# A gated feed-forward's up-projection, with eight block products per unit or seven

## The chip, the cores and the metric

The kernel runs on one core of a Trainium2 chip. The metric is the time of one execution on the device, in microseconds (us). The core has five instruction streams that run side by side and meet at semaphores: TensorE (PE in the profile, its weight loads PEld), VectorE (DVE), ScalarE (ACT), GpSimd (POOL) and SyncE (SP), which issues the DMAs.

## The reference

One layer of a hybrid encoder on 1024 prompt rows and 8 × 16 sample rows, 1152 rows in all, of width 1024. Attention, a pooling branch and gates come first and are not touched. The change is in the feed-forward part:

```python
h2 = rmsnorm(x, norm_ffn)
up = h2 @ w_up                                   # (1152, 1024) @ (1024, 5632)
c, conv_new = causal_dwconv(up, conv_left, conv_w, conv_b)   # width 3 along the rows
gate, val = jnp.split(c, [D_FF], axis=-1)        # D_FF = 2816
x = x + (jax.nn.gelu(gate) * val) @ w_down       # (2816, 1024)
```

All data is float32. The kernel holds each matmul operand as two parts of type fp32r, `hi` (a rounded copy) and `lo` (the rest), and adds three matmuls: hi·hi, hi·lo and lo·hi (`mm3`, lines 120 to 123).

## The kernel before

The stages follow one another: input norm and pooling branch, projections and attention, the sample rows' attention, gates and output projection (to 893 us), up-projection (893 to 1446 us), down-projection (to the end).

The normalised input of the feed-forward lies transposed in SBUF: `mh0`/`ml0` hold rows 0 to 383, `mh12`/`ml12` rows 384 to 1151, each as 8 k-blocks of 128 channels. The up-projection (`up_unit`, lines 1303 to 1333) goes over 22 units m. A unit makes 128 gate columns (u = m) and 128 value columns (u = 22 + m). For each, `load_col` fetches the 1024 × 128 weight block, ACT makes its hi part and POOL its lo part (line 98); TensorE then makes three chunks of 384 rows, in the order 1, 2, 0, each 8 k-blocks × 3 matmuls into a PSUM bank. ACT copies each chunk to E (line 1320) and, scaled, to C (line 1321); DVE adds the two other convolution taps (lines 1324 and 1325, 128 sample and 1024 prompt columns); then GELU on ACT, the product with the value half on DVE (line 1332), and a store to DRAM (`sp_g`). Weight blocks have three buffers.

The down-projection runs over 18 units, one for each half of the 22 g blocks and each tile of 128 rows. Two units share each pass over the weight blocks where blocks are still arriving (units 0 and 1, 7 and 8, 9 and 10); the others run alone. `wd_load` fetches a block of w_down and splits it, `g_load` a tile of g. PSUM there has the tags `tp` and `pj`, two banks each, one tag for each half of the output columns; line 1396 adds a finished half to the residual.

The Tile framework orders the instructions of each engine before the program runs, by its own reckoning and by program order, and places the semaphores. Inside `manual_schedule` the order is the written one; the down-projection has that for TensorE alone, the up-projection not.

Of the kernel before, what the change touches and what calls it, by code (L numbers as in the profile page):

```python
# [25 lines left out]
NU = DFF // P  # L26
# [13 lines left out]
def trunk_kernel(  # L40
# [15 lines left out]
    def f32(ap):  # L56
        return ap.bitcast(F32)

    def mk_pool(name, side=None, space=None, stack=ctx):
        kw = dict(name=name, bufs=1)  # L60
        if space is not None:
            kw["space"] = space
        if side is not None:
            kw["side"] = side
        if space != DRAM:
            kw["reuse_waits"] = "tile"
        return stack.enter_context(tc.tile_pool(**kw))
# [120 lines left out]
        for _, fn in fill[i:]:  # L188
            fn()

    psp = mk_pool("ps", space=PSUM)
    ZT = ("z", 3)
    TT = ("tp", 2)

# [1044 lines left out]
    convp = fcp.tile([P, 4, 2 * NU + 4], F32, name="convp")  # L1239
    convs = fcp.tile([P, 2 * NU, 16], F32, name="convs")  # L1240
    convq = fcp.tile([P, 64, 2], F32, name="convq")[:, :2 * NU, :]


    s5 = ExitStack()
# [57 lines left out]
    EA = -(-EL // HD) * HD  # L1302
    def up_unit(m):
        cc = []
        for s_ in range(2):
            u = s_ * NU + m
            wt = load_col(w_up3, u * P, f"wup{u}")
            E = p6.tile([P, EA], F32, tag="E", bufs=3, name=f"E{u}")
            C = p6.tile([P, T], F32, tag="C", bufs=3, name=f"C{u}")
            pool.memset(E[:, EZ:EP], 0.0)  # L1310
            pool.tensor_copy(E[:, 0:16], sconvT[:, u, :])
            for c in CORD:
                cs = slice(c * CH, (c + 1) * CH)
                ps = psp.tile([P, CH], F32, tag="z", bufs=3, name=f"up{u}_{c}")
# [7 lines left out]
            for tap, sh in ((1, 1), (0, 2)):  # L1322
                wv = convp[:, tap, u:u + 1]
                dve.scalar_tensor_tensor(C[:, 0:P], E[:, 16 - 8 * sh:EZ - 8 * sh], wv, C[:, 0:P], ALU.mult, ALU.add)  # L1324
                dve.scalar_tensor_tensor(C[:, P:T], E[:, EP - sh:EL - sh], wv, C[:, P:T], ALU.mult, ALU.add)  # L1325
            pool.tensor_copy(convs[:, u, :].rearrange("p (b j) -> p j b", j=2),
                             E[:, P:EZ].rearrange("p (j b) -> p j b", b=NB))
            pool.tensor_copy(convq[:, u, :], E[:, EL - 2:EL])
            cc.append(C)
        act.activation(cc[0], cc[0], AF.Gelu_apprx_tanh)  # L1330
        g = p6.tile([P, T], F32, tag="g", bufs=2, name=f"g{m}")
        dve.tensor_tensor(g, cc[0], cc[1], ALU.mult)
        sync.dma_start(sp_g[:, m, :], g)

    def conv_out(rows, n, stores, nm):
        ps = psp.tile([P, P], F32, tag="av", bufs=1, name=f"tr_{nm}")
        tc.keep_in_program_order(pe.transpose(ps[:n, :], rows, ident))
        st = pa.tile([P, P], F32, tag="cst", bufs=2, name=nm)
# [22 lines left out]

    def wd_load(m):
        i = m % NH
        alt = (wp, "hi", "lo", 3) if i < 3 else (pa, "dh", "dl", PA) if i < 3 + PA else \
            (pb, "dh", "dl", NH - 3 - PA)
        src = w_down[0, m * P:(m + 1) * P, :]
        wds[m] = load_w(lambda r: [(r, src)], [D], f"wd{m}", "ad" if i % 2 else "ap", alt)

    def g_load(u, parts=1):
        h, t = UNITS[u]  # L1370
        gq = pa if u % 4 < 2 else pb
        gh, gl = [gq.tile([P, NH, P], F32R, tag=f"gg{i}", bufs=2, name=f"g{u}_{i}") for i in range(2)]
        raw = pa.tile([P, NH, P], F32, tag="graw", bufs=2, name=f"g{u}_r")
# [26 lines left out]
    def final_half(t, hf):  # L1400
        hs = slice(hf * 512, (hf + 1) * 512)
        if hf == 0:
            fin[t] = [p8.tile([P, D], F32, tag=tg, bufs=2, name=f"{tg}{t}") for tg in ("yo", "xg")]
# [16 lines left out]
    for m in range(NU):  # L1420
        up_unit(m)
        if m in (8, 16):
            conv_rows(0, m - 8)
            conv_rows(1, m - 8)
        if m == 17:
            for q in range(3, 3 + PA):
                wd_load(q)
            g_load(0)
            g_load(1)
    s_m.close()  # L1430
    pb = mk_pool("pb", "right")
    for q in (0, 1, 2, *range(3 + PA, NH)):
        wd_load(q)
    s6.close()
    p8 = mk_pool("p8", "left")
    gfin = p8.tile([P, D], F32, name="gfin")
    sync.dma_start(gfin, norm_final.rearrange("(o d) -> o d", o=1).to_broadcast([P, D]))
    xr = [p8.tile([P, D], F32, name=f"xr{t}") for t in range(NT)]
    for t in range(NT):
        sync.dma_start(xr[t], sp_x[t])  # L1440
        if t == 1:
            g_load(2)
            g_load(3)

    with tc.manual_schedule(engines={mybir.EngineType.PE}):
        for u0, n in ((0, 2), *((u, 1) for u in range(2, 7)), (7, 2), (9, 2), *((u, 1) for u in range(11, 18))):
            us = range(u0, u0 + n)
            for u in us:
                if 4 <= u + 2 < len(UNITS):
                    g_load(u + 2)  # L1450
            if n == 2:
                for m in range(NH):
                    for u in us:
                        for hf in range(2):
                            down_mm(u, hf, (m,))
                    if u0 == 7:
                        wd_load(NH + m)
            if u0 == 0:
                conv_rows(0, 16)
                conv_rows(1, 16)  # L1460
                conv_last()
            for u in us:
                for hf in range(2):
                    if n == 1:
                        down_mm(u, hf, range(NH))
                    down_add(u, hf)
                    if u >= NT:
                        final_half(u - NT, hf)
# [32 lines left out]
```

## Time and profile before

| what | value |
|---|---|
| three runs | 1735.52, 1736.49, 1736.60 us, median 1736.49 |
| profiled execution | 1734.46 us, span from first to last instruction 1732.7 us |
| mean granted clock of TensorE | 0.993 |
| TensorE / DVE / ACT / POOL busy | 97% / 46% / 43% / 26% |
| DMA | 160.5 MB, 93 GB/s on average |

Busy matmuls overlap each other, so the spacing of their starts, not their length, says what a stream of them costs.

### The profile page before, as it was taken

What the parts mean: (1) busy time and instruction counts of PE and PEld (TensorE: products, weight loads), DVE (VectorE), ACT (ScalarE), POOL (GpSimd) and SP (SyncE); (2) the same over time, 40 slices, a digit from 0 to 9 for tenths busy, and PEclk for the clock granted to TensorE, in tenths of its full rate; (3) what the DMA queues carried; (4) which work ended last, traced back from release to release, by engine and by line L of the source; (5) the groups of instructions that cost most, each with busy time, mean ns of one, the idle gap of its engine ahead of it and who ended that gap; (6) DMA issues with size and microseconds to landing.
All of it is one profiled execution on the core that took longest, in us unless ns stands there. A gap on an engine that the chain in (4) does not pass through costs nothing.

```text
span 1732.7 us, 24198 instructions
## 1 busy us (share of the span) xinstructions
PE 1683.6 (97%) x9721; PEld 1565.2 (90%) x9721; DVE 790.5 (46%) x1078; ACT 747.6 (43%) x1468; POOL 453.2 (26%) x518
## 2 busy tenths in 40 slices
PE   8999999899899999999999999999999999998998
PEld 7999998889799988888789999999999998887886
DVE  5360026878777776554344343334435344212221
ACT  5331116778777776443334333434334333112211
POOL 5111153121324104224313232223223222002211
PEclk9999999999999999999999999999999999999999
DMA  6112131111213127666312122124213114514311
GB/s 188 50 37 78 64 99 46 49 52 41 60 44 98 60 95 256 216 209 193 118 61 62 65 72 69 52 78 131 76 51 116 64 63 177 160 50 143 87 37 37
DMA packets 164206, 160.51 MB, mean 93 GB/s; under 512 B 8401, under 2 KB 138141, under 8 KB 164093
## 3 DMA queue, kind: packets, MB, share of 16 engines
q1 hardware_dynamic: 164093, 158.96, 28.8%
q8 instruction: 76, 1.25, 0.3%
q14 instruction: 37, 0.30, 0.1%
HBM read 119.32 MB, written 39.35 MB: 92 GB/s over the span
## 4 chain that ended last, share of the span: by engine, by line
PE 76%; DVE 11%; ACT 7%; DMA 3%; issue 2%; POOL 1%; SPq 0%; POOLq 0%; ACTq 0%
PE up L122 11%; PE up L121 11%; PE up L123 11%; PE dn L121 5%; PE dn L122 5%; PE dn L123 5%; DVE S L609 4%; DVE e L610 2%; PE gb L122 2%; PE gb L123 2%; PE gb L121 2%; DVE e L607 2%; PE avs L818 2%; PE zs L788 2%; PE o L122 1%
## 5 line engine op out<-in xcount | busy, mean ns | idle before, releaser
L121 PE MATMUL up<-mh,wup_h 128*128 128x384 f32 x1056 | 353.4, 335 | 0.0
L123 PE MATMUL up<-mh,wup_l 128*128 128x384 f32 x1056 | 352.9, 334 | 0.0
L122 PE MATMUL up<-ml,wup_h 128*128 128x384 f32 x1056 | 352.8, 334 | 0.0
L1324 DVE SCALAR_TENSOR_TENSOR C<-E,convp,C 128x128 f32<-128x128 f32 x88 | 81.3, 924 | 323.2 <-ACT C L1321 314.8
L121 PEld LDWEIGHTS up<-mh,wup_h 128*128 128x128 f32 x1056 | 198.3, 188 | 0.1
L122 PEld LDWEIGHTS up<-ml,wup_h 128*128 128x128 f32 x1056 | 198.3, 188 | 0.0
L123 PEld LDWEIGHTS up<-mh,wup_l 128*128 128x128 f32 x1056 | 198.3, 188 | 0.0
L121 PE MATMUL dn<-wd_h,g 128*128 128x512 f32 x396 | 155.6, 393 | 5.6 <-DVE xr L1396 5.6
L122 PE MATMUL dn<-wd_l,g 128*128 128x512 f32 x396 | 155.2, 392 | 0.0
L123 PE MATMUL dn<-wd_h,g 128*128 128x512 f32 x396 | 155.0, 392 | 0.0
L98 POOL TENSOR_TENSOR wup_l<-wup_r,wup_h 128x1024 fp32r<-128x1024 f32 x44 | 105.3, 2393 | 180.5 <-ACT wup_h L97 180.5
L1320 ACT COPY E<-up 128x384 f32<-128x384 f32 (+2 forms) x176 | 65.7, 399 | 177.4 <-PE up L123 177.4
L1325 DVE SCALAR_TENSOR_TENSOR C<-E,convp,C 128x1024 f32<-128x1024 f32 x88 | 114.1, 1297 | 0.0
L97 ACT CAST wup_h<-wup_r 128x1024 fp32r<-128x1024 f32 x44 | 46.2, 1051 | 116.3 <-PE up L122 113.9
L1396 DVE TENSOR_TENSOR xr<-dn,xr 128x512 f32<-128x512 f32 x36 | 24.6, 689 | 154.0 <-PE dn L123 154.0
L121 PEld LDWEIGHTS dn<-wd_h,g 128*128 128x128 f32 x396 | 75.0, 189 | 21.8 <-DVE xr L1396 6.0
L1321 ACT ACTIVATE C<-up,convp 128x384 f32<-128x384 f32 x132 | 89.9, 681 | 0.0
L123 PEld LDWEIGHTS dn<-wd_h,g 128*128 128x128 f32 x396 | 75.0, 189 | 15.7
L122 PEld LDWEIGHTS dn<-wd_l,g 128*128 128x128 f32 x396 | 75.1, 190 | 15.5
L121 PE MATMUL kv<-wkv_h,hTh 128*128 128x256 f32 x288 | 83.6, 290 | 1.1 <-DVE qz L508 1.1
L123 PE MATMUL kv<-wkv_h,hTl 128*128 128x256 f32 x288 | 81.4, 283 | 0.0
L122 PE MATMUL kv<-wkv_l,hTh 128*128 128x256 f32 x288 | 81.3, 282 | 0.0
(293 smaller groups left out, 3874.6 us busy)
## 6 DMA issues: line engine op xcount, KB each, us to landing
wup_r<-in_w_up_dram SPq DMA_DIRECT2D x44, 512.0 KB
sp_g<-g SPq DMA_DIRECT2D x22, 576.0 KB
g_r<-sp_g SPq DMA_DIRECT2D x18, 704.0 KB
wd_r<-in_w_down_dram SPq DMA_DIRECT2D x22, 512.0 KB
v<-in_cache_v_dram SPq DMA_DIRECT2D x32, 256.0 KB
kr<-in_cache_k_dram SPq DMA_DIRECT2D x7, 1024.0 KB
sp_tb<-tb SPq DMA_DIRECT2D x8, 576.0 KB
out_dram<-kvst SPq DMA_DIRECT2D x72, 64.0 KB
```

Source lines behind the costliest of these rows:

```text
L97: act.copy(hi, raw)
L98: (pool if how[1] == "p" else dve).tensor_tensor(lo, raw, f32(hi), ALU.subtract)
L121: pe.matmul(ps, lhsT=lh, rhs=rh, start=start, stop=False)
L122: pe.matmul(ps, lhsT=lh, rhs=rl, start=False, stop=False)
L123: pe.matmul(ps, lhsT=ll, rhs=rh, start=False, stop=stop)
L607: dve.scalar_tensor_tensor(ev, z, 0.0, ev, ALU.max, ALU.add)
L609: dve.tensor_tensor_scan(Sv[:, ::-1], ev[:, ::-1], ev[:, ::-1], init, ALU.add, ALU.bypass)
L610: dve.tensor_tensor(ev, z, Sv, ALU.subtract)
L1320: act.copy(d_, s2_)
L1321: act.activation(C[:, cs], ps, AF.Identity, scale=convp[:, 2, u:u + 1], bias=convp[:, 3, u:u + 1])
L1324: dve.scalar_tensor_tensor(C[:, 0:P], E[:, 16 - 8 * sh:EZ - 8 * sh], wv, C[:, 0:P], ALU.mult, ALU.add)
L1325: dve.scalar_tensor_tensor(C[:, P:T], E[:, EP - sh:EL - sh], wv, C[:, P:T], ALU.mult, ALU.add)
```

## The change

With H1 the first 576 rows, H2 the last 576, K1 and K2 the two halves of the 1024 input channels, and A the four weight blocks of a unit (gate or value columns by K1 or K2), a unit of the up-projection is a product of a 2 × 2 block matrix with a 2 × 2 block matrix: eight block products. Units 2 to 21 now make it with seven, in the Winograd form of Strassen's algorithm. T1, T2, T3 and T4 are block sums of the input, made once by `t_make` and `t_third` in float32 and split again; T3 overwrites the H2, K1 block in place. S1 to S4 are block sums of the unit's weights, made per unit in float32 (`up_sum`) and split like the plain blocks (`up_w`). The products are added up by DVE from PSUM (`sum_add`, `out_add`) and the convolution reads E as before. Units 0 and 1 keep the old form (`up_plain`). The store takes C itself in place of a tile g, and the value half's convolution of a unit is written behind the first product of the next.

Around it: PSUM is reopened as four double banks for both projections; TensorE's order in both is the written one; the loads of g tiles and of w_down blocks 3 to 5, that stood behind unit 17, now stand behind the last unit, with g tiles and blocks placed where the T tiles and the normalised input lay.

```diff
-    PA = 3
-    pa = mk_pool("pa", "left")
+    s_ps.close()
+    psp = mk_pool("ps2", space=PSUM)
+    tq = mk_pool("tq", "left", stack=s_t)
...
+    H1 = ((mh0, ml0, 0, CH), (mh12, ml12, 0, HB))
+    H2 = ((mh12, ml12, HB, CH), (mh12, ml12, HB + CH, HB))
+    PIECES = ((0, CH), (CH, HB))
+    TQ = {n: [tq.tile([P, KH, HT], F32R, name=f"{n}{i}") for i in range(2)] for n in ("T1", "T2", "T4")}
...
+    def t_split(n, k, x):
+        hi, lo = [t[:, k, :] for t in TQ[n]]
+        act.copy(hi, x)
+        pool.tensor_tensor(lo, x, f32(hi), ALU.subtract)
+
+    def t_make(k):
+        x, y, z_ = [rt(i, f"t{i}_{k}") for i in range(3)]
+        bop(H2, k, x, ALU.subtract, 0, (H1,))
+        bop(H2, k, y, ALU.subtract, 1, (H1,))
+        dve.tensor_tensor(x, x, y, ALU.add)
+        t_split("T1", k, x)
+        bop(H2, KH + k, z_, ALU.subtract, 0, x)
+        bop(H2, KH + k, z_, ALU.add, 1)
+        t_split("T2", k, z_)
+        y = rt(1, f"t4_{k}")
+        bop(H1, KH + k, y, ALU.subtract, 0, z_)
+        bop(H1, KH + k, y, ALU.add, 1)
+        t_split("T4", k, y)
+
+    def t_third(k):
+        y = rt(k % 3, f"t3_{k}")
+        dve.tensor_tensor(y, f32(TQ["T2"][0][:, k, :]), f32(TQ["T2"][1][:, k, :]), ALU.add)
+        bop(H1, k, y, ALU.subtract, 0)
+        bop(H1, k, y, ALU.subtract, 1)
+        for j, (o, c) in enumerate(PIECES):
+            th, tl, o2, _ = H2[j]
+            act.copy(th[:, k, o2:o2 + c], y[:, o:o + c])
+            dve.tensor_tensor(tl[:, k, o2:o2 + c], y[:, o:o + c], f32(th[:, k, o2:o2 + c]), ALU.subtract)
...
+    PROD = (("A11", "B11"), ("A12", "B21"), ("S2", "T2"), ("S3", "T3"), ("S1", "T1"), ("S4", "B22"), ("A22", "T4"))
...
+    def up_w(m, i):
...
+        hi, lo = [t[:, ks, :] for t in w["t"]]
+        act.copy(hi, src)
+        pool.tensor_tensor(lo, src, f32(hi), ALU.subtract)
...
+    def product(m, i):
...
+        for j, (o, c) in enumerate(PIECES):
+            ps = acc[:, j, :c]
+            for k in range(KH):
...
+                mm3(ps, hi[:, k, :], lo[:, k, :], rh, rl, k == 0, k == KH - 1)
...
+    def out_add(ps, r_, E, half):
+        for j, a, b, d_ in e_parts(E, half):
+            o = PIECES[j][0]
+            dve.tensor_tensor(d_, ps[:, j, a:b], r_[:, o + a:o + b], ALU.add)
+
+    def sum_add(d_, ps, r_):
+        for j, (o, c) in enumerate(PIECES):
+            dve.tensor_tensor(d_[:, o:o + c], ps[:, j, :c], r_[:, o:o + c], ALU.add)
...
+    NORD = 2
     with tc.manual_schedule(engines={mybir.EngineType.PE}):
+        t_make(0)
+        up_plain(0)
+        for i in range(1, KH):
+            t_make(i)
+        for m in range(1, NORD):
+            up_plain(m)
+        up_raw(NORD)
+        for n in ("S1", "S2", "S3", "S4"):
+            up_sum(NORD, n)
+        for i in range(6):
+            up_w(NORD, i)
+        for i in range(KH):
+            t_third(i)
+        for m in range(NORD, NU):
+            up_fast(m)
...
+        for u in range(2):
+            g_load(u)
+        for q in range(NH):
+            wd_load(q)
...
     def down_mm(u, hf, ms):
         h, t = UNITS[u]
-        if (u, hf) not in dps:
-            tag = ("tp", "z", "pj", "z", "tp", "z", "pj", "z")[(2 * u + hf) % 8] if u in (0, 1) else \
-                ("tp", "pj")[hf]
-            dps[u, hf] = psp.tile([P, 512], F32, tag=tag, bufs=3 if tag == "z" else 2, name=f"dn{u}_{hf}")
+        if (u, 0) not in dps and hf == 0:
+            ps = ps2(f"dn{u}")
+            dps[u, 0], dps[u, 1] = ps[:, 0, :], ps[:, 1, :]
```

## Rows read from the trace of the kernel before

**Rows 1.** The page: busy time, share of the span and instructions.

```profile
PE 1683.6 (97%) x9721; PEld 1565.2 (90%) x9721; DVE 790.5 (46%) x1078; ACT 747.6 (43%) x1468; POOL 453.2 (26%) x518
```

**Rows 2.** By stretch: length; PE, PEld, DVE, ACT, POOL busy; clock; DMA share, GB/s.

```profile
893.00:1446.00 553.00, 552.39 (x3193) 550.95 (x3191) 219.91 (x206) 218.41 (x388) 158.59 (x220) 1.00 0.23 74
1446.00:1583.00 137.00, 136.30 (x603) 112.32 (x602) 42.28 (x36) 28.45 (x29) 21.00 (x9) 1.00 0.44 140
1583.00:1596.00 13.00, 7.45 (x21) 5.62 (x20) 6.22 (x5) 5.67 (x5) 4.72 (x2) 0.74 0.50 153
1462.00:1477.00 15.00, 14.65 (x66) 11.86 (x64) 4.18 (x6) 3.74 (x4) 2.39 (x1) 1.00 1.00 385
```

**Rows 3.** Timeline of PE: start, length; 13 spacings of 384 columns lie between.

```profile
999.72 0.33 PE L121 MATMUL up<-mh,wup_h 128*128 128x384 f32 x1
...
1001.97 0.33 PE L122 MATMUL up<-ml,wup_h 128*128 128x384 f32 x1
```

**Rows 4.** Timeline of PE, 20 spacings of 256 columns.

```profile
261.57 0.28 PE L121 MATMUL kv<-wkv_h,hTh 128*128 128x256 f32 x1
...
263.97 0.28 PE L123 MATMUL kv<-wkv_h,hTl 128*128 128x256 f32 x1
```

**Rows 5.** Timeline of PE: two matmuls of 128 columns and the next.

```profile
298.07 0.22 PE L677 MATMUL av<-ah,vhl 128*128 128x128 f32 x1
298.13 0.27 PE L678 MATMUL av<-al,vhl 128*128 128x128 f32 x1
298.24 0.45 PE L634 MATMUL z<-kk,qd 128*128 128x512 f32 x1
```

**Rows 6.** Timeline of PEld: the weight loads of the last two.

```profile
298.07 0.19 PEld L678 LDWEIGHTS av<-al,vhl 128*128 128x128 f32 x1
298.18 0.19 PEld L634 LDWEIGHTS z<-kk,qd 128*128 128x128 f32 x1
```

**Rows 7.** Timeline of POOL at the end of the up stage.

```profile
1447.45 2.41 POOL L98 TENSOR_TENSOR wd_l<-wd_r,wd_h 128x1024 fp32r<-128x1024 f32 x1 [4.39 <-ACT wd_h L97]
...
1450.02 3.44 POOL L98 TENSOR_TENSOR wd_l<-wd_r,wd_h 128x1024 fp32r<-128x1024 f32 x1
```

**Rows 8.** Timeline of DVE in the same stretch.

```profile
1449.93 1.27 DVE L1325 SCALAR_TENSOR_TENSOR C<-E,convp,C 128x1024 f32<-128x1024 f32 x1
1451.13 2.48 DVE L1324 SCALAR_TENSOR_TENSOR C<-E,convp,C 128x128 f32<-128x128 f32 x1
1453.53 1.27 DVE L1325 SCALAR_TENSOR_TENSOR C<-E,convp,C 128x1024 f32<-128x1024 f32 x1
1454.73 1.61 DVE L1376 TENSOR_TENSOR g<-g_r,g 128x1408 fp32r<-128x1408 f32 x1
```

**Rows 9.** Groups by form, DVE: busy, mean ns; idle before. From PSUM, then SBUF.

```profile
L442 DVE TENSOR_TENSOR tb<-bb,tb 128x384 f32<-128x384 f32 x24 | 13.4, 558 | 98.6 <-PE bb L123 98.6
...
L1407 DVE TENSOR_TENSOR xg<-xr,gfin 128x512 f32<-128x512 f32 x9 | 6.2, 690 | 0.2
```

**Rows 10.** Groups by form, POOL.

```profile
L98 POOL TENSOR_TENSOR wup_l<-wup_r,wup_h 128x1024 fp32r<-128x1024 f32 x44 | 105.3, 2393 | 180.5 <-ACT wup_h L97 180.5
...
L1407 POOL TENSOR_TENSOR xg<-xr,gfin 128x512 f32<-128x512 f32 x9 | 12.0, 1337 | 58.7 <-DVE xr L1396 58.6
```

**Rows 11.** Chain of waits near 1560 us: start, length, what.

```profile
1557.70 0.23 PE dn L122
...
1558.19 1.06 ACT wd_h L97
...
1560.53 4.47 DMA wd_r<-in_w_down_dram
...
1565.07 1.06 ACT wd_h L97
```

**Rows 12.** Timeline of PE around its wait between down units 8 and 9.

```profile
1589.60 0.80 PE L121 MATMUL dn<-wd_h,g 128*128 128x512 f32 x1 [5.55 <-DVE xr L1396]
...
1595.65 0.39 PE L123 MATMUL dn<-wd_h,g 128*128 128x512 f32 x1
```

More of the change, by code (lines that the diff above doesn't have):

```diff
@@ L189, in weave @@
             fn()
-    psp = mk_pool("ps", space=PSUM)
+    s_ps = ExitStack()
+    psp = mk_pool("ps", space=PSUM, stack=s_ps)
     ZT = ("z", 3)
@@ new lines, in rt @@
+    def rt(i, nm):
+        return p6.tile([P, HT], F32, tag=("r1", "r5", "r2")[i], bufs=1, name=nm)
+    def t_split(n, k, x):
[15 more added lines that the diff above has]
+        t_split("T4", k, y)
@@ new lines, in taps @@
+    def taps(u, E, C):
+        for tap, sh in ((1, 1), (0, 2)):
+            wv = convp[:, tap, u:u + 1]
+            dve.scalar_tensor_tensor(C[:, 0:P], E[:, 16 - 8 * sh:EZ - 8 * sh], wv, C[:, 0:P], ALU.mult, ALU.add)
+            dve.scalar_tensor_tensor(C[:, P:T], E[:, EP - sh:EL - sh], wv, C[:, P:T], ALU.mult, ALU.add)
+        pool.tensor_copy(convs[:, u, :].rearrange("p (b j) -> p j b", j=2),
+                         E[:, P:EZ].rearrange("p (j b) -> p j b", b=NB))
+        pool.tensor_copy(convq[:, u, :], E[:, EL - 2:EL])
@@ new lines, in conv_all, with gate_store, ps2 @@
+    def conv_all(u, E):
+        C = p6.tile([P, T], F32, tag="C", bufs=3, name=f"C{u}")
+        for d_, s_ in ((C[:, 0:P], E[:, 16:EZ]), (C[:, P:T], E[:, EP:EL])):
+            act.activation(d_, s_, AF.Identity, scale=convp[:, 2, u:u + 1], bias=convp[:, 3, u:u + 1])
+        taps(u, E, C)
+        return C
+    def gate_store(m, cg, cv):
+        act.activation(cg, cg, AF.Gelu_apprx_tanh)
+        dve.tensor_tensor(cg, cg, cv, ALU.mult)
+        sync.dma_start(sp_g[:, m, :], cg)
+    def ps2(nm):
+        return psp.tile([P, 2, 512], F32, tag="X", bufs=4, name=nm)
@@ L1321, in up_unit @@
                 act.activation(C[:, cs], ps, AF.Identity, scale=convp[:, 2, u:u + 1], bias=convp[:, 3, u:u + 1])
[L1322 to L1327, printed above, removed]
@@ L1328, in up_unit @@
-            pool.tensor_copy(convq[:, u, :], E[:, EL - 2:EL])
-            cc.append(C)
[L1330 to L1333, printed above, removed]
+            taps(u, E, C)
+            cc.append(C)
+        gate_store(m, *cc)
+    PROD = (("A11", "B11"), ("A12", "B21"), ("S2", "T2"), ("S3", "T3"), ("S1", "T1"), ("S4", "B22"), ("A22", "T4"))
@@ new lines, in trunk_kernel, with up_raw, up_sum @@
+    BLK = {"B11": (H1, K1), "B21": (H1, K2), "B22": (H2, K2), "T3": (H2, K1)}
+    raws = {}
+    wts = {}
+    def up_raw(m):
+        raws[m] = []
+        for s_ in range(2):
+            u = s_ * NU + m
+            raw = wp.tile([P, KD, P], F32, tag="raw", bufs=2, name=f"wup{u}_r")
+            sync.dma_start(raw, w_up3[:, :, u * P:(u + 1) * P])
+            raws[m].append(raw)
+    def up_sum(m, n):
+        rg, rv = raws[m]
+        w = wts.setdefault(m, {})
+        w[n] = p6.tile([P, KH, P], F32, tag="st", bufs=4, name=f"{n}_{m}")
+        a, b, op = {"S1": (rv[:, K1, :], rv[:, K2, :], ALU.add), "S2": (w.get("S1"), rg[:, K1, :], ALU.subtract),
+                    "S4": (rg[:, K2, :], w.get("S2"), ALU.subtract),
+                    "S3": (rg[:, K1, :], rv[:, K1, :], ALU.subtract)}[n]
+        dve.tensor_tensor(w[n], a, b, op)
@@ new lines, in up_w @@
+    def up_w(m, i):
+        n = PROD[i][0]
+        rg, rv = raws[m]
+        w = wts.setdefault(m, {})
+        src = w[n] if n[0] == "S" else {"A11": rg[:, K1, :], "A12": rg[:, K2, :], "A22": rv[:, K2, :]}[n]
+        if i % 2 == 0:
+            w["t"] = [wp.tile([P, KD, P], F32R, tag=tg, bufs=3, name=f"wup{m}_{i}_{tg}") for tg in ("hi", "lo")]
+        ks = (K1, K2)[i % 2]
+        hi, lo = [t[:, ks, :] for t in w["t"]]
+        act.copy(hi, src)
+        pool.tensor_tensor(lo, src, f32(hi), ALU.subtract)
+        w[i] = (hi, lo)
@@ new lines, in product @@
+    def product(m, i):
+        bn = PROD[i][1]
+        acc = ps2(f"up{m}_{i}")
+        hi, lo = wts[m][i]
+        for j, (o, c) in enumerate(PIECES):
+            ps = acc[:, j, :c]
+            for k in range(KH):
+                if bn in BLK:
+                    half, ks = BLK[bn]
+                    th, tl, o2, _ = half[j]
+                    kk = k + (KH if ks is K2 else 0)
+                    rh, rl = th[:, kk, o2:o2 + c], tl[:, kk, o2:o2 + c]
+                else:
+                    rh, rl = [t[:, k, o:o + c] for t in TQ[bn]]
+                mm3(ps, hi[:, k, :], lo[:, k, :], rh, rl, k == 0, k == KH - 1)
+        return acc
@@ new lines, in e_parts @@
+    def e_parts(E, half):
+        if half == 0:
+            return ((0, 0, P, E[:, 16:EZ]), (0, P, CH, E[:, EP:EP + CH - P]),
+                    (1, 0, HB, E[:, EP + CH - P:EP + HT - P]))
+        o = EP + HT - P
+        return ((0, 0, CH, E[:, o:o + CH]), (1, 0, HB, E[:, o + CH:o + HT]))
+    def out_add(ps, r_, E, half):
[3 more added lines that the diff above has]
+    def sum_add(d_, ps, r_):
+        for j, (o, c) in enumerate(PIECES):
+            dve.tensor_tensor(d_[:, o:o + c], ps[:, j, :c], r_[:, o:o + c], ALU.add)
@@ new lines, in trunk_kernel, with up_fast @@
+    pend = {}
+    def up_fast(m):
+        nxt = m + 1 if m + 1 < NU else None
+        for i in range(7):
+            ps = product(m, i)
+            if i == 0:
+                r1 = rt(0, f"r1_{m}")
+                for j, (o, c) in enumerate(PIECES):
+                    act.copy(r1[:, o:o + c], ps[:, j, :c])
+                up_w(m, 6)
+                if "g" in pend:
+                    pend.pop("g")()
+            elif i == 1:
+                eg = e_tile(m)
+                out_add(ps, r1, eg, 0)
+                if nxt is not None:
+                    up_raw(nxt)
+            elif i == 2:
+                sum_add(r1, ps, r1)
+            elif i == 3:
+                r2 = rt(2, f"r2_{m}")
+                sum_add(r2, ps, r1)
+                if nxt is not None:
+                    up_w(nxt, 0)
+                    up_w(nxt, 1)
+                    up_sum(nxt, "S1")
+                    up_sum(nxt, "S2")
+            elif i == 4:
+                ev = e_tile(NU + m)
+                out_add(ps, r2, ev, 1)
+                sum_add(r1, ps, r1)
+                if nxt is not None:
+                    up_sum(nxt, "S3")
+                    up_sum(nxt, "S4")
+            elif i == 5:
+                out_add(ps, r1, eg, 1)
+                if nxt is not None:
+                    up_w(nxt, 2)
+                    up_w(nxt, 3)
+                cg = conv_all(m, eg)
+            else:
+                out_add(ps, r2, ev, 0)
+                if nxt is not None:
+                    up_w(nxt, 4)
+                    up_w(nxt, 5)
+                pend["g"] = lambda: gate_store(m, cg, conv_all(NU + m, ev))
@@ L1335, in conv_out @@
     def conv_out(rows, n, stores, nm):
-        ps = psp.tile([P, P], F32, tag="av", bufs=1, name=f"tr_{nm}")
-        tc.keep_in_program_order(pe.transpose(ps[:n, :], rows, ident))
-        st = pa.tile([P, P], F32, tag="cst", bufs=2, name=nm)
+        ps = ps2(f"tr_{nm}")[:, 0, :P]
+        pe.transpose(ps[:n, :], rows, ident)
+        st = cst.tile([P, P], F32, tag="cst", bufs=2, name=nm)
         act.copy(st[:n, :], ps[:n, :])
@@ L1402, in final_half @@
         if hf == 0:
-            fin[t] = [p8.tile([P, D], F32, tag=tg, bufs=2, name=f"{tg}{t}") for tg in ("yo", "xg")]
+            fin[t] = [p8.tile([P, D], F32, tag=tg, bufs=n_, name=f"{tg}{t}") for tg, n_ in (("yo", 2), ("xg", 1))]
         yo, xg = fin[t][:2]
```

81 lines of the change are left out of this document (46 added, 35 removed).

## The prediction

> **What bounds the kernel now.** I read the page first, then a table by stage, then single spacings. The page says that TensorE is busy for 97% of the span [rows 1]. The table by stage puts the up-projection at 893 to 1446 us: TensorE busy for 552.4 of 553.0 us at full clock, DVE for 220, ACT for 218, POOL for 159 [rows 2]. The stage is therefore worth what its matmuls cost, and the other three engines are covered work with room. The change is judged by two questions: what the new matmul stream costs, and whether the covers still hold once DVE and POOL get the block sums.
>
> A busy matmul overlaps the next one, so I price by starts. In the stage a 384-column matmul starts every (1001.97 − 999.72)/13 = 0.173 us [rows 3]; a 256-column one elsewhere every (263.97 − 261.57)/20 = 0.120 us [rows 4]. That is 0.053 us for 128 columns.
>
> **The new stream.** An old unit is 2 × 3 chunks × 8 k-blocks × 3 = 144 matmuls of 384 columns, 144 × 0.1733 = 24.96 us. A new one is 7 products × 4 k-blocks × 3 × 2 pieces: 84 of 384 and 84 of 192 columns. The columns fall by an eighth, but the instructions rise from 144 to 168. No matmul of 192 columns is in the trace. The line through rows 3 and 4 gives 0.093 us. Against it stands the weight load, which every matmul has of its own. Where two 128-column matmuls of the same type follow each other, the second starts 0.06 us after the first, but the next one 0.11 us later [rows 5]; the loads beside them start 0.11 us apart, each matmul some 0.06 us after its own load began [rows 6]. So a load takes the port for 0.108 us, starts no earlier than the matmul before its own, and a run of 192-column matmuls (0.093) outruns it. The first few go at 0.093, the later ones at 0.108: the thirteenth start lies 12 × 0.108 − 0.05 = 1.25 us after the first, 0.104 each. I take that; the bounds are 0.093 and 0.110. A product is 12 × 0.1733 + 1.25 = 3.33 us, a unit 23.3 us, and 20 units save 20 × (24.96 − 23.3) = **33 us** (bounds 51 and 23).
>
> The Trainium skill (TensorE: Matmul & The Clock Gate, section LDWEIGHTS) puts a load at its columns divided by 1.2, so 107 ns for 128, which this trace's 0.11 us agrees with; its rule alone, 0.107 for every short matmul, would make the saving an estimated 29 us.
>
> **The covers in the steady state.** DVE work per new unit: the taps, 4 × (1.20 + 0.3) = 6.0 us by starts [rows 8]; the gate product 1.36 (a line between the rows' shapes: 0.155 us + 1.04 ns a column [rows 9]); four block sums of 512 columns at 0.69, 2.8 us. These 10.2 us read two SBUF operands. Seven products come out of PSUM by adds of 384 + 192 columns (0.56 + 0.36), five times, and of 128 + 256 + 192 (0.29 + 0.42 + 0.36) twice: 6.7 us. Total 16.9 of 23.3 us. POOL: seven low parts of 512 columns at 1.3 us [rows 10], 9.1 us, and its small copies at most 2.4 us (the 53 us of the stage besides the low parts, over 22 units [rows 2, 10]).
>
> The two engines are not independent. At 1450.02 POOL's 1024-column subtract, elsewhere 2.39 us, took 3.44: it stood behind the DVE instruction begun at 1449.93 [rows 7, 8, 10]. At 1451.13 DVE's 128-column tap took 2.48 instead of 0.3, to the end of that subtract [rows 8]. A DVE instruction with two SBUF operands and POOL's subtract exclude each other for their whole length; adds out of PSUM keep 0.56 us beside POOL and are free of it [rows 9]. The Trainium skill (SBUF — State Buffer, section Who interferes with whom) states the same as an exclusive lock, and the trace agrees. So the shared port carries 10.2 + 11.5 = 21.7 us per 23.3 us, DVE 16.9. It holds, with 7% to spare. I price it at nothing; if POOL's work falls wholly on DVE's waits, it is a rival below.
>
> **The T blocks, made under two old units.** This work comes once, all of it on the shared port. One k-block of T1, T2, T4: six pairs of 384 + 192 columns and one 576 (0.76) on DVE, 6.3 us, and three 576-column subtracts on POOL (1.44), 4.3 us; four k-blocks, 42 us. T3: 4 × (0.76 + 3 × 0.92) = 14.1. Queued among them: three of the four halves' taps and one gate product, 10.4; on POOL one 1024-column low part 2.4, four of 512 columns 5.2, copies 3; the first unit's sums 2.8. Sum 80 us. From 1447.45 to 1454.80 the alternating instructions took 7.35 us where their own lengths sum to 7.9 [rows 7, 8], so × 0.93: 75 us. TensorE's cover is two old units and three products before the one that needs T3: 49.9 + 10 = 60 us. It stalls **15 us**. Bounds: everything that may wait moved behind T3, 71 us of work, gives 6; the last half's taps, its product and two more weights in front, and no overlap, give 27. A stall costs clock too: after the 5.55 us wait at 1583.7, 14 matmuls took 6.05 us instead of 3.2, the granted clock of that stretch being 0.74 [rows 2, 12]: **3 us**.
>
> At the seam before the first unit TensorE's order is now fixed, so up matmuls no longer fill between the last transposes; that is at most one 24-matmul block (4.2 us): **2 us**.
>
> **The start of the down-projection.** Before, w_down's blocks 3 to 5 and two g tiles were loaded while the up stage ran, and TensorE was busy for 136.3 of the next 137 us [rows 2]. Now these tiles lie where T1 to T4 and m lie, and the first g load waits for products to end. The first g also needs ACT and DVE (1.61 us a tile), and DVE first serves the last taps: before, one such subtract ran at 1454.73, 8.5 us into the down stage [rows 8], unhurt because nothing waited. I take 5 us to the first matmul (3 to 12). Then a pair of weight blocks takes one round of cast, subtract and load, 1565.07 − 1558.19 = 6.9 us, 3.45 a block, where TensorE eats one in 12 × 0.23 = 2.7 us [rows 11]. Only two blocks can be ahead; the eleventh is ready 3.4 + 4 × 6.9 = 31 us in, just when wanted (5 + 27). But eight blocks, ten half-megabyte tiles (xr, gfin) and four g tiles, 12 MB, share DMA that gave 385 GB/s when full [rows 2]: 32 us for the same 30. I add 5 us (0 to 10) and 1 of clock: **11 us** (3 to 22).
>
> **What PSUM gives back.** At 1583.7, between down units 8 and 9, TensorE waited 5.55 us for DVE's add, because the two buffers of each half were taken; DVE stood behind a weight block's subtract [rows 12]. With four double buffers units 9 and 10 find free ones: **−8.5 us** with its clock (0 if another wait stands there).
>
> **Sum.** −33 + 2 + 15 + 3 + 11 − 8.5 = −10.5 on the profiled execution's 1734.5 us, which lies 2 us under the median of the runs. Against 1736.5: **1726 us**.
>
> **Rivals.** (1) *The covers hold*: other work goes behind T3 and the stall stays at 6 us or below with its clock, or short matmuls cost 0.093: −33 + 2 + 6 + 2 + 5 − 8.5 = −26.5, 1710 us, down to 1692 with both. For it: DVE and POOL each have room by the stage table. Against: the exclusion in rows 7 and 8. (2) *The shared port becomes the bound in every unit, and the kernel is slower.* DVE's 16.9 plus POOL's 11.5 × 0.93, if no subtract runs beside an add from PSUM, is 27.6 us; it decides from where more than 6.4 us of POOL's 11.5 fall on DVE's waits. At 24.9 us a unit, little more than a third of the way, the saving is gone and the sum is 0 + 2 + 18 + 11 − 8.5 = +22: 1759 us. For it: 93% load of the port. Against: 6.7 us of adds and 6.4 us of idle DVE in which POOL can run. (3) *No gain that counts*: short matmuls at 0.110, saving 23 us, or the 8.5 us not given back: 1735 to 1737.
>
> **Chances.** The forecast, 1714 to 1732 us, 0.35; rival 1 0.20; rival 3 0.13; rival 2, or milder forms of it with the long ends of both stalls, 0.32. About 0.2%, 3.5 us, is what a measurement tells from no change: faster 0.55, same 0.13, slower 0.32. Eight in ten: 1697 to 1760.
>
> **What would show it.** Spacing of the short matmuls 0.10 to 0.11 us; units 2 to 21 at 23.3 us with TensorE busy; one wait of about 15 us in unit 2 before the product of T3, ended by DVE; DVE taps and POOL subtracts longer than their own lengths; a wait of some us before the first dn matmul; none near the end of unit 8. Wrong, if units take 24 us or more (rival 2), or if unit 2 does not wait (rival 1).

## The result, and the profile after

The changed kernel takes **1782.13 us** (median of 4 runs, 1781.31 to 1786.17) beside 1736.01 us of the kernel before on the same chip: ratio 1.027, interval [1.025, 1.029], slower by some 46 us. The forecast was 1726 us, the range ended at 1760: wrong in sign and outside its range. The profiled span is 1781.1 us against 1732.7, 48.4 us more, and the two traces differ as follows.

The page's busy line, to be held against [rows 1]: TensorE is busy for nearly the same time as before, in a longer span. So the time went into waits, and the saving in matmuls is not to be seen in the total.

```profile
PE 1680.1 (94%) x10201; PEld 1554.6 (87%) x10201; DVE 994.6 (56%) x1558; ACT 746.4 (42%) x1428; POOL 552.8 (31%) x630
```

By stretch, with the columns of [rows 2]: the two old units, the first new one, the other 19, the passage to the down-projection, the down-projection.

```profile
902.00:959.00 57.00, 53.77 (x291) 53.14 (x292) 53.67 (x73) 23.84 (x43) 32.36 (x27) 0.94 0.09 29
959.00:992.00 33.00, 27.10 (x167) 26.79 (x167) 25.94 (x51) 11.93 (x25) 12.37 (x16) 0.90 0.16 51
992.00:1458.00 466.00, 459.47 (x3202) 458.38 (x3200) 329.72 (x549) 168.88 (x268) 207.79 (x281) 1.00 0.22 69
1458.00:1483.00 25.00, 0.10 (x1) 0.00 (x0) 12.07 (x13) 9.96 (x10) 7.88 (x4) 0.57 0.62 186
1483.00:1774.00 291.00, 277.97 (x1191) 224.87 (x1191) 74.34 (x75) 55.87 (x77) 45.58 (x42) 0.98 0.31 98
```

The waits of TensorE in the up- and the down-projection (total, times, longest):

```profile
PE dn L121 <- ACT g L1566: 25.1, 1, 25.1
PE dn L121 <- DVE xr L1586: 11.4, 12, 2.7
...
PE up L121 <- ACT C L1406: 6.2, 3, 3.0
PE up L121 <- DVE r L1478: 5.8, 4, 2.9
...
PE up L121 <- ACT cs L1532: 3.6, 2, 1.8
```

Where the 48.4 us are, each a difference of the two traces:

| place | us |
|---|---|
| start of the up-projection: 902.7, before worth 897.3 (its end less 22 units of 24.96; 23 of its matmuls stood between the last transposes) | +5.4 |
| units 0 to 2: 26.2, 30.3 and 33.2 us, over two of 24.96 and one of 24.03 | +15.8 |
| 20 units at their undisturbed 24.03 us in place of 24.96 | −18.6 |
| waits inside units 9 to 18 | +9 |
| passage: TensorE idle for 25.1 us, before not at all | +25.1 |
| down-projection, first to last matmul: 291.2 us, before 279.6 | +11.6 |

Not all of the first row is the seam: the last matmul of the output projection starts at 894.0 us, before at 892.3, and up to there the code is the same. And some 1.1 us of the second row are not the block sums: unit 0 starts at the lower clock behind the waits of the last transposes, and it takes 26.1 us without any block sum too (the first experiment).

**The stream.** One product, at the seam of its two pieces, and the weight loads beside it:

```profile
1040.48 0.36 PE L121 MATMUL up<-mh,wup_hi 128*128 128x384 f32 x1
1040.68 0.34 PE L122 MATMUL up<-ml,wup_hi 128*128 128x384 f32 x1
...
1042.60 0.25 PE L121 MATMUL up<-mh,wup_hi 128*128 128x192 f32 x1
1042.68 0.28 PE L122 MATMUL up<-ml,wup_hi 128*128 128x192 f32 x1
...
1043.91 0.36 PE L121 MATMUL up<-mh,wup_hi 128*128 128x384 f32 x1
```

```profile
1042.60 0.19 PEld L122 LDWEIGHTS up<-ml,wup_hi 128*128 128x128 f32 x1
1042.71 0.19 PEld L123 LDWEIGHTS up<-mh,wup_lo 128*128 128x128 f32 x1
```

Twelve short matmuls take 1043.91 − 1042.60 = 1.31 us, 0.109 each; only the first starts early. The loads follow each other at 0.11 us. And the first long matmul behind a short one costs 0.20 instead of 0.173. So a product is 1043.91 − 1040.48 = 3.43 us, not 3.33, and a unit 24.03, not 23.3.

**The passage.** SP's queue at the end of the up-projection; a group's length runs from its first issue to its last:

```profile
1446.89 25.16 SPq L106 DMA_DIRECT2D wd_r<-in_w_down_dram  x6
1472.10 0.42 SPq L1385 DMA_DIRECT2D sp_g<-C  x1
1472.98 0.33 SPq L106 DMA_DIRECT2D wd_r<-in_w_down_dram  x1
1473.36 2.97 SPq L1565 DMA_DIRECT2D g_r<-sp_g  x2
```

The two g loads that the first matmul needs are issued at 1473.4, behind seven weight blocks, all but the first of which wait for a raw buffer, and behind the last unit's store, whose gate product had been ready since 1469.5. In the written program the g loads stand ahead of the weight blocks; the framework's own order put them behind.

**The down-projection.** One of twelve places where TensorE waits, in the middle of a unit:

```profile
1557.46 0.39 PE L123 MATMUL dn<-wd_h,g 128*128 128x512 f32 x1
1557.88 0.69 DVE L1586 TENSOR_TENSOR xr<-dn,xr 128x512 f32<-128x512 f32 x1 [4.67 <-PE dn L123]
...
1558.63 0.50 PE L121 MATMUL dn<-wd_h,g 128*128 128x512 f32 x1 [0.79 <-DVE xr L1586]
```

The first half ends, DVE adds it to the residual, and only then the second half's first matmul starts, though it writes another bank.

### The profile page after: what moved, and what is told of

The parts are those of the page before. It is cut to its first block, busy times and chain, and to the rows that moved or that the text cites. A ratio compares the mean times of both kernels' runs of the same rounds, so it can differ in the third digit from the quotient of the medians.

```text
span 1781.1 us, 25959 instructions
## 1 busy us (share of the span) xinstructions
PE 1680.1 (94%) x10201; PEld 1554.6 (87%) x10201; DVE 994.6 (56%) x1558; ACT 746.4 (42%) x1428; POOL 552.8 (31%) x630
## 3 DMA queue, kind: packets, MB, share of 16 engines
q8 instruction: 80, 1.31, 0.3%
## 5 line engine op out<-in xcount | busy, mean ns | idle before, releaser
L121 PE MATMUL up<-mh,wup_hi 128*128 128x384 f32 (+1 forms) x640 | 194.8, 304 | 3.6 <-ACT cs L1532 3.6
L123 PE MATMUL up<-mh,wup_lo 128*128 128x384 f32 (+1 forms) x640 | 195.3, 305 | 0.0
L122 PE MATMUL up<-ml,wup_hi 128*128 128x384 f32 (+1 forms) x640 | 195.0, 305 | 0.0
L121 PE MATMUL dn<-wd_h,g 128*128 128x512 f32 x396 | 157.4, 398 | 37.5 <-ACT g L1566 25.1
L121 PE MATMUL up<-T,wup_hi 128*128 128x384 f32 x480 | 147.9, 308 | 8.8 <-DVE r L1478 5.8
L122 PE MATMUL dn<-wd_l,g 128*128 128x512 f32 x396 | 155.7, 393 | 0.0
L123 PE MATMUL up<-T,wup_lo 128*128 128x384 f32 x480 | 147.6, 308 | 0.0
L122 PE MATMUL up<-T,wup_hi 128*128 128x384 f32 x480 | 147.6, 308 | 0.0
L121 PEld LDWEIGHTS up<-mh,wup_hi 128*128 128x128 f32 x640 | 121.5, 190 | 4.0 <-ACT cs L1532 4.0
L122 PEld LDWEIGHTS up<-ml,wup_hi 128*128 128x128 f32 x640 | 121.5, 190 | 0.0
L123 PEld LDWEIGHTS up<-mh,wup_lo 128*128 128x128 f32 x640 | 121.4, 190 | 0.0
L1444 POOL TENSOR_TENSOR wup_lo<-S,wup_hi 128x512 fp32r<-128x512 f32 x80 | 103.8, 1318 | 27.5 <-ACT wup_hi L1443 27.5
L121 PEld LDWEIGHTS up<-T,wup_hi 128*128 128x128 f32 x480 | 92.1, 192 | 9.8 <-ACT wup_hi L1443 5.7
L122 PEld LDWEIGHTS up<-T,wup_hi 128*128 128x128 f32 x480 | 92.1, 192 | 0.0
L123 PEld LDWEIGHTS dn<-wd_h,g 128*128 128x128 f32 x396 | 75.2, 190 | 17.3 <-DVE g L1567 1.4
```

Of the source, the lines that this page charges most:

```text
L121: pe.matmul(ps, lhsT=lh, rhs=rh, start=start, stop=False)
L122: pe.matmul(ps, lhsT=lh, rhs=rl, start=False, stop=False)
L123: pe.matmul(ps, lhsT=ll, rhs=rh, start=False, stop=stop)
L1444: pool.tensor_tensor(lo, src, f32(hi), ALU.subtract)
```

## The experiments

Each was timed against the kernel before in runs of its own; the changed kernel's 1.027 stands for some 1781 us in each. "The changed kernel" is the one above. Nearly to the end of the output projection, it and all kernels made from it run the same instructions in the same order, yet the last matmul of that stage starts anywhere from 888.5 to 895.8 us in their traces. A few us between two kernels need not be the edit's; where it matters, I count from that matmul.

**All units in the old form.** `up_fast` is never called:

```diff
-        t_make(0)
-        up_plain(0)
...
+        for m in range(NU):
+            up_plain(m)
```

> All 22 units in the old form of eight block products; the block sums T1 to T4 and the seven products are left out, while the order written out for TensorE, the two-bank PSUM tiles, the later loads of g and the down-projection stay as in the changed kernel. If the loss sits in what surrounds the products (5.4 us at the start, 15 to 25 us between up- and down-projection, 11.6 us in the down-projection, as the two traces differ): 1765 to 1780 us. If the loss comes with the algebra itself (block sums, more work for VectorE behind the last product): 1740 to 1750 us.

Measured: 1769.5 us, ratio 1.021 [1.019, 1.022].

```profile
PE dn L121 <- ACT g L1566: 18.4, 1, 18.4
PE dn L121 <- DVE xr L1586: 11.3, 12, 2.7
```

36 of the 46 us are lost without a single one of the seven products: the passage (18.4 us idle) and the down-projection stand in this kernel too. The first theory holds. But it also says that the seven products, as the changed kernel cuts them, gain nothing: with them it takes some 11 us more. In the two traces their up-projection is 4.6 us longer and the passage behind it 6.7.

**g loads early on SP's queue.** The last unit's gate tile lies in a place of its own (`clast`), so that its store can be written later:

```diff
-        for u in range(2):
-            g_load(u)
-        for q in range(NH):
+        for q in range(2):
             wd_load(q)
+        for u in range(2):
+            g_load(u, tc.keep_in_program_order)
+        for q in range(2, NH):
+            wd_load(q, tc.keep_in_program_order)
+            if q == 3:
+                tc.keep_in_program_order(sync.dma_start(sp_g[:, NU - 1, :], clast))
```

> The changed kernel, but the first two loads of g stand on SP's queue right behind the loads of the first two weight blocks, and the last store of sp_g behind the fourth block. If the 25.1 us between the stages are the place of these loads in SP's queue: a gap of 7 to 12 us and 1765 to 1771 us. If the weight blocks limit the start anyway: the gap shrinks, but the first pair of units is longer by as much, and the time stays at 1777 to 1783 us.

Measured: 1766.3 us, ratio 1.019 [1.017, 1.021], 15 us less.

```profile
1451.12 1.18 SPq L1567 DMA_DIRECT2D g_r<-sp_g  x2
1452.39 4.90 SPq L106 DMA_DIRECT2D wd_r<-in_w_down_dram  x2
1466.21 0.33 SPq L1645 DMA_DIRECT2D sp_g<-clast  x1
```

```profile
1463.46 0.80 PE L121 MATMUL dn<-wd_h,g 128*128 128x512 f32 x1 [5.39 <-ACT g L1568]
...
1469.92 0.79 PE L123 MATMUL dn<-wd_h,g 128*128 128x512 f32 x1 [5.24 <-DVE g L1569]
```

The loads go out at 1451, while the last products run, 22 us earlier. The place in the queue was the cause. What is left are two waits of 5 us: the cast and the subtract of g stand on ACT and DVE behind the last unit's convolution.

**A tile for each half.** In the single units of the down-projection:

```diff
+        elif (u, hf) not in dps:
+            dps[u, hf] = ps2(f"dn{u}_{hf}")[:, 0, :]
```

> The changed kernel, but in the single units of the down-projection each half has a PSUM tile of its own in place of one bank of a shared tile of two. If the 0.78 us at each unit's middle are a wait of the second half for the add that reads the first half of the same tile: 12 waits go, 9 to 10 us, and the time is 1771 to 1774 us. If the four tiles come free too late, whoever shares them: 1780 to 1784 us.

Measured: 1764.8 us, ratio 1.018 [1.016, 1.020], 16 us less: more than expected.

```profile
1486.00:1760.00 274.00, 272.22 (x1191) 224.09 (x1191) 74.07 (x76) 55.73 (x76) 45.58 (x42) 0.99 0.33 105
```

All twelve waits are gone, the longest, 2.7 us, among them, and the stage takes 273.7 us, 17.5 less; the waits' own sum is 11.4, the rest lies in slower first matmuls behind each wait and in stretches at the lower clock. The wait was made by two halves sharing a tile, not by a lack of tiles. And 273.7 is 5.9 us below the kernel before: the gift that I had forecast was there, under this wait.

**Even pieces.** Five of the seven products cut 576 columns in halves:

```diff
+    HE = HT // 2
+    EVEN = ((0, HE), (HE, HE))
+    def pieces(i):
+        return PIECES if i in (0, 1) else EVEN
```

> The changed kernel, but five of the seven products cut their 576 columns into 288 and 288 in place of 384 and 192 (the two that read the block lying over two tiles stay). If the short matmul is held at 0.111 us by its weight load and one of 288 columns by its columns (0.133 us, between the 0.120 us of 256 and the 0.1735 us of 384 columns): 24 times 0.133 for 12 times 0.1735 and 12 times 0.111, 0.22 us less a product, 22 us over 100 products: 1758 to 1763 us. If every matmul of such a product carries a like extra: 0 to 5 us less, 1777 to 1782 us.

Measured: 1740.6 us, ratio 1.004 [1.003, 1.006], 41 us less, twice the expectation.

```profile
1064.08 0.29 PE L121 MATMUL up<-mh,wup_hi 128*128 128x288 f32 x1
...
1066.46 0.29 PE L121 MATMUL up<-T,wup_hi 128*128 128x288 f32 x1
```

18 spacings in 2.38 us, 0.132 each: the price that the columns give, so the short matmul's 0.109 is a floor and no general surcharge. Units take 22.78 us, 25 us over 20 units. The rest was not in the expectation: most of the waits in units 9 to 18 are gone (8 us), for a reason that no run shows, and unit 2 takes 28.9 in place of 33.2. Of the 42 us between the two traces the up-projection has 36; 3 lie ahead of it, in what was not changed.

**Another order inside a product.** Short and long matmuls alternate:

```diff
+            for n_, (w, x) in enumerate(((hi, 0), (hi, 1), (lo, 0))):
+                for j, (o, c) in enumerate(PIECES):
+                    pe.matmul(acc[:, j, :c], lhsT=w[:, k, :], rhs=r_[j][x], ...)
```

> The changed kernel with another order inside each product: the 384-column and the 192-column matmul of the same weights follow one another, so that short and long alternate. If a weight load can start only with the matmul before its own, the long matmul behind a short one pays what the short one behind a short one paid, and the pair stays at 0.285 us: 1779 to 1786 us. If loads run ahead and hide under the long matmul: the pair falls to 0.1735 + 0.093, 0.22 us less a product, 30 us over 140 products: 1748 to 1758 us.

Measured: 1783.9 us, ratio 1.029 [1.027, 1.031], no change. Each row is a pair of 384 and 192:

```profile
1041.12 0.45 PE L1463 MATMUL up<-mh,wup_hi 128*128 128x384 f32 x2
1041.41 0.46 PE L1463 MATMUL up<-ml,wup_hi 128*128 128x384 f32 x2
```

A pair takes 0.29 us in this order too. In the rows of the stream above, load L122 starts with the matmul before its own, both at 1042.60; since this order gains nothing, a load does not run further ahead than one matmul here.

**The three together.** 

> The three edits that each took time off the changed kernel, together: g loads early in SP's queue (-15), a PSUM tile for each half in the single units (-17), even pieces (-41). If the three losses stand apart in time and each was wholly its own: 1782 - 73 = 1709 us, 1705 to 1713. If one wait covers another (the down-projection's start, once early, waits for weight blocks): 1716 to 1730 us.

Measured: 1714.1 us, ratio 0.988 [0.986, 0.989], 5 us above the plain sum, faster than the kernel before. The losses stand nearly apart.

**Old algebra, repaired surroundings.** All units in the old form, with early g loads and a tile for each half. 

> All 22 units in the old form of eight block products (block sums and seven products left out) with two of the repairs: early g loads and a PSUM tile for each half in the single units. It stands to the three repairs together (1714 us, ratio 0.988) as the old algebra to the new one in the same surroundings. If seven products are worth what the unit times say (20 units of 22.8 in place of 25.0 us, 44 us, less 12 us of stall at the block sums): 1742 to 1750 us. If the repairs alone made the gain and the algebra none: 1712 to 1720 us.

Measured: 1743.4 us, ratio 1.005 [1.003, 1.006]. Beside the three together (0.988) the seven products, evenly cut, are worth 29 us, the stall of their block sums already taken off (by the traces, 31.0 us in the up-projection less 2.9 in the passage). Repairing the surroundings alone does not beat the kernel before.

**The start of the up-projection.** On top of the three, the first unit uses the old PSUM tiles and stands ahead of the written order:

```diff
-    s_ps.close()
-    psp = mk_pool("ps2", space=PSUM)
...
+    up_plain(0)
+    s_ps.close()
+    psp = mk_pool("ps2", space=PSUM)
     with tc.manual_schedule(engines={mybir.EngineType.PE}):
```

> As the three together, and the first unit's products use the old PSUM tiles, the change to the two-bank tiles stands behind that unit. If the 5 us at the start of the up-projection come from that change of the PSUM pool (no up matmul can stand between the last transposes, because its tile waits for theirs): up matmuls stand between the transposes again and the time is 4 to 6 us below the three together. If they come from the order written out by hand alone, or the transposes' own waits for VectorE remain the limit: within 1.5 us of it.

Measured: 1714.2 us, ratio 0.989 [0.986, 0.991], no difference.

```profile
895.17 0.66 PE L150 MATMUL tr_f<-ident,xnf 128*128 128x128 f32 x4
895.58 0.43 PE L121 MATMUL up<-mh,wup_h 128*128 128x384 f32 x1
```

Up matmuls do stand between the transposes again, but most of the time came back one unit later: the longest wait for `ACT C` in the first units is 6.5 us, in the three together 3.0. Counted from the last matmul of the output projection, the last up matmul ends after 525.7 us, there after 527.9; so some 2 us are left, fewer than the times show. With the block sums the limit, an earlier start of TensorE is in the main an earlier wait.

**Four old units.** On top of that, a quarter of the block sums behind each of four:

```diff
+    NORD = 4
...
+        t_make(0)
+        for m in range(1, NORD):
+            up_plain(m)
+            t_make(m)
```

> As the one before, but four units in the old form in place of two, with one quarter of the block sums T1, T2 and T4 behind each. If the stall of the first units is VectorE with too much to do in too little time: in the even-piece run it was 12.2 us (0.4, 5.6 and 6.2 us over 25.0, 25.0 and 22.8 us); the two added old units cost 2 times 2.2 us; T3, which can only be made behind the last old unit, keeps 3 to 6 us of stall; 2 to 5 us less than the one before. If the stall is T3 alone: 3 to 5 us more than the one before.

Measured: **1706.2 us**, ratio **0.984 [0.982, 0.985]**, the best of all. It is 8 us below the one before, but of the 7.2 us between the two traces 4.4 lie ahead of the up-projection, in what was not changed. Counted from there the last up matmul ends after 522.8 us, 2.9 earlier: what the first theory expected. Its longest waits from 890 us on:

```profile
PE up L121 <- ACT C L1414: 6.2, 2, 5.3
PE dn L121 <- ACT g L1577: 5.3, 1, 5.3
PE dn L123 <- DVE g L1578: 5.2, 1, 5.2
```

**Two tries at what is left there.** First the low parts of the first g tiles on GpSimd, `(pool if u < 2 else dve).tensor_tensor(gl, ...)`. 

> As the one before, and the low parts of the first two units' g are subtracted on GpSimd in place of VectorE. If the second wait at the down-projection's start (5.2 us in the run with early g loads) is VectorE busy with the last up unit when the low part is wanted: 2 to 3 us less than the one before. If GpSimd's longer subtraction (by its 1024 columns, 2.4 us and so some 3.3 us for 1408) and the weight blocks behind it on GpSimd take it back: within 1 us of it.

Measured: 1713.5 us, ratio 0.987 [0.986, 0.989], 7 us more, 5 of them in the down-projection (284.3 us from first to last matmul, 279.3 in the run above); the rest lies ahead of the up-projection. GpSimd is then late for the weight blocks that follow it in its queue:

```profile
PE dn L122 <- POOL wd_l L98: 5.2, 4, 1.5
PE dn L123 <- POOL g L1578: 3.2, 2, 2.0
```

Then, without that, the high parts of the block sums on DVE, `dve.tensor_copy(hi, x)` in `t_split`. 

> As the run with four units in the old form, but the high parts of the block sums T1, T2 and T4 are cast on VectorE in place of ScalarE. If the 5.3 us wait that is left in the second unit is ScalarE's queue (its cast of a block sum waits for VectorE, and the copies that free the PSUM tile stand behind that cast): the wait and the half clock after it go, 6 to 9 us, 1697 to 1701 us. If VectorE has too much to do in these units whoever casts (12 casts more, some 0.6 us each): 1704 to 1711 us.

Measured: 1712.2 us, ratio 0.987 [0.985, 0.990], 6 us more. The wait in the second unit, unit 1, is gone: that unit takes 24.96 us, in the run above 32.2. But a longer wait with the same releaser stands in unit 2, and units 0 to 3 together are 5 us longer. Here are the wait, the stretch that it ends (with the columns of [rows 2]) and what ACT did just before:

```profile
PE up L121 <- ACT C L1414: 10.3, 1, 10.3
```

```profile
928.00:966.00 38.00, 27.86 (x161) 27.54 (x159) 37.34 (x54) 6.73 (x12) 19.03 (x18) 0.90 0.13 44
```

```profile
964.01 1.16 ACT L1389 ACTIVATE C<-C 128x1152 f32<-128x1152 f32 x1 [18.50 <-DVE C L1376]
```

ACT stands idle for 18.5 us at the GELU, which waits for DVE's taps, and the copies that free the PSUM tile stand behind it on ACT's queue. In the run above ACT stood for 8.15 us at a cast of a block sum, at 939.25 us, which waited for DVE as well. So the place of the wait changed and what it waits for did not: DVE, busy for 37.3 of 38 us, is the limit of these units, and the second theory holds, 1 us beyond its range. How much of DVE's time is waiting for GpSimd's subtracts, no run shows. The same with three old units. 

> As the run with the high parts cast on VectorE, but three units in the old form in place of four, the last two quarters of the block sums both behind the third. If VectorE now has room: 2 us less, a unit of 25.0 us becomes one of 22.8. If the block sums then come late again for the first new unit: 3 to 8 us more.

Measured: 1711.5 us, ratio 0.988 [0.986, 0.989], no clear difference from four. The wait is the same 10.3 us in unit 2. By the units the first theory holds: unit 3, now a new one, takes 22.8 us in place of 25.0, without a wait, and units 0 to 3 together take 113.9 us in place of 116.2.

**The waits inside units 9 to 18.** In one kernel the transposes of the convolution rows moved behind the last unit, and `up_raw(nxt)` went ahead of the pinned store. 

> The changed kernel with two edits: the four transposes of the convolution rows that stand behind units 8 and 16 are moved behind the last unit, and on SP's queue each unit's store of sp_g stands behind both loads of the next unit's weights instead of between them. If the waits of units 9 and 17 (1.8 us each) are the two-bank tiles that the transposes take, and those of units 12, 15, 16 and 18 are VectorE's block sums waiting for the late second weight load: units 3 to 21 all take 24.0 to 24.2 us and the time is 8 to 10 us less, 1771 to 1775 us. If VectorE is simply full in some units: the waits of units 12 to 18 stay, 1777 to 1780 us.

Measured: 1789.7 us, ratio 1.032 [1.029, 1.034], 8 us more. Waits inside units 3 to 21 by the changed kernel, then by this one:

```profile
PE up L121 <- ACT cs L1532: 3.6, 2, 1.8
PE up L121 <- DVE r L1478: 2.9, 3, 1.4
```

```profile
PE up L121 <- DVE r L1478: 9.5, 9, 2.5
```

The waits behind the transposes, for `ACT cs`, are gone, so those were theirs; unit 17 takes 24.5 us in place of 26.2. Unit 9 takes 27.8 all the same, with one of the other waits, and those grew: the store's place on SP's queue was not their cause. The second weight load goes out 17.3 us behind the first with the store between them (1206.77 and 1224.05 us) and behind them (1211.62 and 1228.89). In the changed kernel DVE's queue stood like this in unit 12:

```profile
1229.64 0.69 DVE L1432 TENSOR_TENSOR S<-wup_r 128x512 f32<-128x512 f32 x1 [5.09 <-DMA wup_r<-in_w_up_dram]
...
1232.24 1.54 DVE L1478 TENSOR_TENSOR r<-up,r 128x384 f32<-128x384 f32 x4
```

DVE stands idle for 5.09 us before a weight sum that waits for a load, and the adds that free PSUM tiles stand behind it. So only that order was changed, `up_sum` moved behind the adds of the fifth product and pinned there. 

> The changed kernel, but VectorE's four weight sums S1 to S4 for the next unit stand behind all adds of the products three to five, which free their PSUM tiles; they are pinned there. If the waits of units 12, 15, 16 and 18 are the adds standing behind the sums, which wait for the second weight load: those units take 24.0 to 24.1 us, units 9 and 17 keep their 26.1 us, 4 to 6 us less, 1775 to 1778 us. If the sums then come late for the next unit's third product, or VectorE is full: 1781 us or more.

Measured: 1780.9 us, ratio 1.026 [1.025, 1.028]. Waits inside units 3 to 21:

```profile
PE up L121 <- ACT cs L1530: 1.9, 2, 1.0
```

Units 12 to 18 all take 24.0 to 24.2 us, except unit 17 with its transposes: the order on DVE's queue was the cause. The time is as before all the same: unit 2 took 39.2 us in place of 33.2, where the sums of the first new unit, pinned too, stand among the block sums on DVE, and TensorE waits 9.3 us for a weight made from them. So the second theory holds as well, at that unit.

## Why the prediction was wrong

Held against the terms of the sum, what PSUM gives back is 20 us off, the stream and the start of the down-projection 14 us each, the waits in units 9 to 18 9 us, the seam 3, and the block sums −2.

**The stream: right mechanism, wrong size.** −33 was forecast, −18.6 measured. The step that failed is the price of a run of short matmuls, 0.104 us each with the first few at 0.093: one of twelve goes early, the run costs 0.109, and the long matmul behind it pays for the last load. The measured product is 0.10 us over the one forecast; 140 of them are 14 us. The row that I should have taken as it stood was the 128-column pair, 0.11 us [rows 5]; the line through the widths of 256 and 384 [rows 3, 4] does not reach below the load. The Trainium skill's rule for a load (TensorE: Matmul & The Clock Gate, section LDWEIGHTS, columns divided by 1.2, which gives 107 ns for 128) agrees with the loads' spacing of 0.11 us and was nearer to the measured 0.109 than my sum.

**The T blocks: right in size, not in form.** 15 us of stall and 3 of clock were forecast; 15.8 were measured, and 14.6 without unit 0. It came not as one wait before T3 but as four of 0.5 to 3 us in units 1 and 2, 9.1 in all, with half clock behind three of them; that the sum is so near is in part luck. More work for DVE in these units made the wait longer, and DVE's taps are longer beside GpSimd's subtracts (2.45 us for 1024 columns at 929.76, elsewhere 1.27), as the forecast's reckoning of the two would have it.

**The seam: 2 forecast, 5.4 measured.** Of these, 1.7 lie ahead of it, and the low clock of unit 0 adds some 1.1. Taking the seam back gained no more than some 2 us while the block sums are the limit.

**The passage: the step that failed was the time to the first matmul.** "I take 5 us to the first matmul (3 to 12)" became 25.1, beyond the bound. I had costed the memory that g waits for and the work of ACT and DVE on it, but not the place of its load on SP's queue, though the diff moved these loads behind the last unit. Seven weight blocks and a store stood in front; that the g loads are written first did not help. Early loads took 15 us off, and the 5.4 us to the first matmul that are then left are the figure that I had taken. A second wait of 5.2 us follows it, so the start costs twice my price even then. The 5 us that I added for the weight blocks did not come: TensorE waits for none of them in the changed kernel's down-projection, and with early loads for one, 0.3 us.

**What PSUM gives back: a gain forecast, a loss found.** −8.5 was forecast, +11.6 measured. The 5.55 us wait of [rows 12] did go. The step failed where four double buffers were taken as eight banks: both halves of a unit share one tile, and the second half waits for the add that reads the first. With a tile for each half the stage is 5.9 us shorter than before.

**The covers.** In the 19 later units DVE and GpSimd kept pace: DVE was busy for 17.4 us a unit and POOL for 10.9, where 16.9 and 11.5 were forecast, TensorE was busy for 459.5 of 466 us, and with even pieces the units ran at 22.78 us. My sign for rival 2, units of 24 us or more, was a bad one: they took 24.03, and the short matmuls alone brought them there. Rival 2, the shared port in every unit, is refuted as the cause of the loss, though the kernel is slower as it said. The waits in units 9 to 18 came from the order of queues, DVE's and TensorE's own with the transposes, not from a full engine; this was in no part of the forecast, which put such waits at nothing.

So the idea is worth 29 us against the old form in like surroundings when the pieces are cut evenly; as the changed kernel cuts them it cost some 11. The larger part of the loss, 36 us, stands at three places that need none of the algebra, and that no sum of busy times shows: the seam, the passage and the halves of the down-projection.

## What to carry to other kernels

Cut pieces evenly before counting columns: where each matmul loads its own weights, a piece narrower than the load (0.11 us here, by an estimate some 230 columns on the line through 256 and 384) costs as much as the load. When a change moves a transfer, write down what then stands ahead of it on its queue and what each of those waits for; the busy shares show nothing of it. A tile was the unit of waiting for the framework here: halves that are finished at different times want tiles of their own, even where they lie in different banks. And before a few us between two kernels are explained, look where in the two traces they lie; up to 7 us lay in stretches that no edit had touched.

## What the runs showed of the hardware

A matmul with its own 128-column weight load has a floor of 0.109 to 0.11 us: 192 columns cost 0.109, 128 cost 0.11 [rows 5], while 288 cost 0.132, on the line through 256 and 384. Alternating narrow and wide matmuls does not get below the floor: the pair of 384 and 192 took 0.29 us in either order. And the half clock behind a wait is not small change: three waits of 3 us in units 1 and 2 brought three stretches at the lower level (1.2 GHz), and these two units took 14.6 us longer than undisturbed ones, with waits of 9.1 in all; the passage left the granted clock at 0.57 over its 25 us.
